# A transformer block on one core: where moving weights lie in SBUF, modulo 256 bytes

## The chip, the core and the metric

The kernel runs on one core of a Trainium2 chip. The metric is the device time of one execution in microseconds (us). Engines are named as in the profile: PE is the matmul engine (TensorE), PEld its loading of stationary operands, ACT is ScalarE, DVE VectorE, POOL GpSimd, SP SyncE. A matmul has a stationary operand (128x128 here, loaded by an instruction LDWEIGHTS) and a moving operand (up to 512 columns), and accumulates into a PSUM bank.

## The reference

One block of a hybrid encoder on 256 rows of width 2048, in float32. Cut to its matrix products:

```python
mem_n = rms_norm(mem, mem_norm_g)
h = rms_norm(x, norm_g[l, 0])
q, k, v, g, lr, u_f, u_h, u_s = jnp.split(h @ w_in[l], split_at, axis=-1)
mix = jnp.concatenate([y_a, y_b, y_c, y_d], axis=-1)
x = x + mix @ w_out[l]
x = x + cross_attention(rms_norm(x, norm_g[l, 1]), mem_n, w_xq[l], w_xkv[l], w_xo[l])
x = x + swiglu(rms_norm(x, norm_g[l, 2]), w_gate_up[l], w_down[l])
return rms_norm(x, final_norm_g)
```

y_a to y_d are four mixers of a quarter of the width each: gated linear attention, a Fourier transform, long convolutions and a short convolution. The products with weights (w_in, w_xkv, w_out, w_xq, w_xo, w_gate_up with 2 x 5632 columns, w_down) make up nearly all of the work.

## The kernel before

**Three products for one.** Every float32 operand a is split into a high part (rounded to the type float32r) and the rest: a = ah + al. A product of two is taken as ah bh + al bh + ah bl, in float32r.

**The stream of weights.** All weights lie in one array W in the order of use: blocks of 128x128, sixteen to a slab of 128x2048 (1 MB), loaded by one DMA from SP into one of three buffers `raw`. `Stream._half` (line 77) takes half a slab, 8 blocks: ACT casts it to `wh` (line 104), DVE subtracts to get `wl` (line 105). `Stream.take` hands out the parts, two or three halves ahead of their use. The tiles `wh` and `wl` have 1088 columns of 4 bytes, of which 1024 are used, from column `at` on (lines 99 to 101). `at` is 0 for blocks in the ranges `ROWS` and 8 for all others.

**Two forms of product.**

- Weights stationary (`mm`, line 304, and `gemm`): wh is loaded, and the activation's slot, 512 columns of which 256 are the high part and 256 the rest, moves past it (line 311); then wl with the high part alone (line 312). A narrow variant splits the first into two of 256 columns (lines 308 and 309).
- Weights moving (`part_rows`, line 353, and `gemm_rows`), called row products below: 128 columns of the activation's high part are loaded and 512 columns of wh move (line 356), then the same with wl (line 357), then the activation's rest with wh (line 358). It is used for the values of the cross-attention, for the values of the gated linear attention, for gate and up, and for down: `ROWS` (line 39) holds their block numbers, 256 + 64 + 2112 = 2432 of 4032. A call for 4 blocks makes 6 matmuls.

**The end.** The last 32 blocks (`HELD`) are not put into the buffers wh and wl but into 16 tiles `held` of their own (lines 88 to 97), in a pool `hp` that `mlp` opens after gate and up (line 752), so that the last products of down can run first for the upper rows and then for the lower ones.

**Places.** Every tile has an address in its SBUF partition. `gap` (line 215) allocates some bytes that nobody uses, so that what follows lies elsewhere; there are several such gaps. In the compiled program of before, the starts of the tiles that matter are, modulo 256 bytes:

| tile | role | remainder |
|---|---|---|
| act, f, oex (activation slots, 2048 bytes each) | stationary in row products, moving past stationary weights | 128 |
| wh, wl (4352 bytes each, 17 x 256) in all 8 buffers, column 0 | moving in row products | 192 |
| wh, wl from column 8 on (32 bytes) | stationary | 224 |
| held (2048 bytes each, after a gap of 64 bytes) | moving | 192 |
| tabh, tabl, backh, backl, hs (Hyena's tables and filters) | stationary on lines 987, 1055, 1056 | 64 |
| w3h, w3l (2048 bytes each) | moving on lines 987, 1055, 1056 | 64 |

The slices that a single matmul takes start at multiples of 512 bytes within these, so they have the remainders of the table.

**Order around it.** Work that is not a weight product (convolutions, attention, norms) is put between the products by a planner (`Background`), which estimates times of PE and DVE; it doesn't depend on addresses. Hyena's transforms are such work: `triple` (line 984) issues three matmuls on line 987, moving w3h, w3l, w3h past stationary tabh, tabh, tabl, each 512 columns wide, and `dft` calls it twice in a row; lines 1055 and 1056 issue two matmuls with w3h and w3l past hs. They stand between the matmuls of row products.

Of the kernel before, what the change touches and what calls it, by code (L numbers as in the profile page):

```python
# [38 lines left out]
ROWS = ((256, 512), (704, 768), (NBLK - 48 * FT, NBLK))  # L39
# [23 lines left out]
class Stream:  # L63
# [13 lines left out]
    def _half(self):  # L77

        nc, n = self.nc, 8 * len(self.halves)
        if n % 16 == 0:  # L80
            self.raw = self.rawp.tile([P, 2048], F32, name="raw", tag="raw")
            for a, b in zip(CUTS[n], CUTS[n][1:]) if n in CUTS else [(0, 1024), (1024, 2048)] if self.after else [(0, 2048)]:
                (nc.scalar if (n, a) == (0, 0) else nc.sync).dma_start(self.raw[:, a:b], self.W[n // 16][:, a:b])
                if self.after:
                    self.after.pop(0)()
        o = (n % 16) * P
        r = self.raw[:, o:o + 1024]
        if n >= NBLK - HELD:
            parts = []
            for a in (0, 512):  # L90
                wh, wl = self.places.pop(0)
                nc.scalar.copy(wh, r[:, a:a + 512])
                nc.vector.tensor_tensor(out=wl, in0=r[:, a:a + 512], in1=wh.bitcast(F32), op=ALU.subtract)
                parts.append((wh, wl))
            self.bg.dve(1024)
            self.halves.append(parts)
            return
        pool = self.extra if self.extra and len(self.halves) % 4 == 3 else self.wp
        wh, wl = (pool.tile([P, 1088], F32R, name=t, tag=t) for t in ("wh", "wl"))
        at = 0 if any(a <= n < b for a, b in ROWS) else 8  # L100
        wh, wl = wh[:, at:at + 1024], wl[:, at:at + 1024]
        edges = [0, 256, 512, 1024] if n == 0 else [0, 512, 1024] if n == 8 else [0, 1024]
        for a, b in zip(edges, edges[1:]):
            nc.scalar.copy(wh[:, a:b], r[:, a:b])  # L104
            nc.vector.tensor_tensor(out=wl[:, a:b], in0=r[:, a:b], in1=wh[:, a:b].bitcast(F32), op=ALU.subtract)  # L105
        self.bg.dve(1024)
        self.halves.append((wh, wl))
# [60 lines left out]
class Block:  # L168
# [576 lines left out]
    def mlp(self):  # L745
        tc, nc, act = self.tc, self.nc, self.act
        with tc.tile_pool(name="fp", bufs=1) as fp:
            self.gap(fp, 192)
            f = act[4:12] + [fp.tile([P, 512], F32R, name=f"f{i}") for i in range(20)] + self.h3
            with tc.tile_pool(name="gp", bufs=2) as gp:  # L750
                self.gate_up(gp, f)
            with tc.tile_pool(name="hp", bufs=1) as hp:
                self.gap(hp, 64)
                held = [hp.tile([P, 512], F32R, name=f"held{i}") for i in range(HELD // 2)]
                self.st.places = list(zip(held[0::2], held[1::2]))
                self.down(f)
# [705 lines left out]
```

## Time and profile before

| | us |
|---|---|
| median of 3 runs | 1491.95 (1491.54 to 1491.97) |
| the profiled execution, its own time | 1492.38 |
| its span in the trace | 1490.6 |
| mean granted clock of TensorE | 0.998 of full |
| DMA, mean over the span | 205 GB/s |

The page gives busy times for each engine, the chain of work that ended last, and groups of instructions: line, engine, operation, what it writes and reads by the program's names (`pg<-wh,act` is written to a PSUM bank pg from wh and act), shapes, count, busy time and mean duration. The span's time counts from 0. Matmuls are pipelined: one starts before the one ahead of it has ended by its record, so the distance from start to start, called pace below, is shorter than the duration, and the sum of durations is more than the time that they take. In the order of time, each row has start, duration, engine, line and operands.

### The profile page before, as it was taken

To read this page: it belongs to the slowest core of one execution; us is meant where nothing else is said; L and a number is where in the kernel's file an instruction comes from. 1 tells how busy PE (TensorE), PEld (TensorE's weight loads), DVE (VectorE), ACT (ScalarE), POOL (GpSimd) and SP (SyncE) were. 2 spreads that over 40 slices of the span, in tenths; PEclk is the share of its full clock that TensorE was granted. 3 is DMA by queue.
4 is the path that set the end of the run, shared out by engine and by line. 5 is a ranking of instruction groups with operands and counts; after the bars stand their busy time and mean duration, and the time that the engine had idled before them with its cause. 6 is when DMAs were issued, how large, how long until landed. Compare 5 with 4: busy or idle time off the path is not lost.

```text
span 1490.6 us, 19837 instructions
## 1 busy us (share of the span) xinstructions
PE 1479.3 (99%) x7586; PEld 1254.6 (84%) x7586; DVE 942.3 (63%) x1379; ACT 767.6 (51%) x1147; POOL 150.1 (10%) x260
## 2 busy tenths in 40 slices
PE   9999999999999999999999999999999999999997
PEld 8888888899899888888888888888888888888886
DVE  6687768778777777877765554555555456444444
ACT  6566655458555556756544444444444445434344
POOL 0100100000000001100052410111110112000000
PEclk9999999999999999999999999999999999999999
DMA  9966554454446555544567766666666666555554
GB/s 348 361 248 210 199 193 164 168 188 145 163 150 228 188 196 205 192 151 170 197 198 241 231 215 218 221 213 218 215 213 212 211 217 230 188 187 191 197 197 141
DMA packets 56174, 306.11 MB, mean 205 GB/s; under 512 B 9197, under 2 KB 10510, under 8 KB 24464
## 3 DMA queue, kind: packets, MB, share of 16 engines
q1 hardware_dynamic: 45632, 281.11, 54.3%
q0 software_dynamic: 10016, 23.08, 4.9%
q8 instruction: 59, 0.97, 0.3%
q10 hardware_dynamic: 432, 0.66, 0.1%
q14 instruction: 35, 0.29, 0.1%
HBM read 291.18 MB, written 13.63 MB: 204 GB/s over the span
## 4 chain that ended last, share of the span: by engine, by line
PE 96%; ACT 1%; DVE 1%; DMA 0%; issue 0%; SPq 0%; ACTq 0%
PE pg L311 21%; PE pg L357 17%; PE pg L358 17%; PE pg L356 17%; PE pg L312 11%; PE pm L357 1%; PE pm L356 1%; PE pm L358 1%; PE pm L987 1%; PE pm L311 1%; PE pg L308 1%; PE pg L309 1%; PE pm L738 1%; PE pm L711 0%; PE pm L312 0%; DMA raw<-in_W 0%
## 5 line engine op out<-in xcount | busy, mean ns | idle before, releaser
L105 DVE TENSOR_TENSOR wl<-raw,wh 128x1024 fp32r<-128x1024 f32 (+1 forms) x503 | 611.8, 1218 | 476.8 <-ACT wh L104 470.1
L104 ACT CAST wh<-raw 128x1024 fp32r<-128x1024 f32 (+1 forms) x503 | 525.1, 1045 | 584.2 <-PE pg L358 397.9
L311 PE MATMUL pg<-act,wh 128*128 128x512 f32 x1296 | 456.0, 394 | 1.1 <-ACT wh L104 0.9
L312 PE MATMUL pg<-act,wl 128*128 128x256 f32 x1472 | 412.2, 280 | 0.2 <-DVE wl L105 0.2
L358 PE MATMUL pg<-wh,act 128*128 128x512 f32 x1008 | 396.1, 393 | 0.0
L357 PE MATMUL pg<-wl,act 128*128 128x512 f32 x1008 | 395.7, 393 | 0.0
L356 PE MATMUL pg<-wh,act 128*128 128x512 f32 x1008 | 392.7, 390 | 0.0
L311 PEld LDWEIGHTS pg<-act,wh 128*128 128x128 f32 x1296 | 243.3, 188 | 54.7 <-ACT wh L104 1.4
L312 PEld LDWEIGHTS pg<-act,wl 128*128 128x128 f32 x1472 | 276.8, 188 | 1.5 <-DVE wl L105 0.5
L356 PEld LDWEIGHTS pg<-wh,act 128*128 128x128 f32 x1008 | 189.2, 188 | 43.5 <-issue 0.4
L357 PEld LDWEIGHTS pg<-wl,act 128*128 128x128 f32 x1008 | 189.3, 188 | 42.6
L358 PEld LDWEIGHTS pg<-wh,act 128*128 128x128 f32 x1008 | 189.4, 188 | 38.7
L780 POOL DMA_DIRECT2D hidden<-u x88 | 57.1, 656 | 311.6 <-DVE u L777 310.1
L308 PE MATMUL pg<-act,wh 128*128 128x256 f32 x176 | 50.0, 284 | 0.0
L309 PE MATMUL pg<-act,wh 128*128 128x256 f32 x176 | 49.5, 281 | 0.0
L357 PE MATMUL pg<-wl,f 128*128 128x512 f32 x120 | 47.3, 394 | 0.0
L356 PE MATMUL pg<-wh,f 128*128 128x512 f32 x120 | 47.0, 392 | 0.0
L358 PE MATMUL pg<-wh,f 128*128 128x512 f32 x120 | 46.6, 388 | 0.0
L196 DVE TENSOR_TENSOR tmp<-pg,tmp 128x256 f32<-128x256 f32 x86 | 36.0, 419 | 8.4 <-ACT tmp L318 6.6
L824 POOL DMA_DIRECT2D xrows<-tmp x48 | 27.7, 586 | 130.0 <-DVE tmp L821 126.2
L318 ACT COPY tmp<-pg 128x256 f32<-128x256 f32 x85 | 30.9, 365 | 9.5 <-PE pg L312 8.3
L308 PEld LDWEIGHTS pg<-act,wh 128*128 128x128 f32 x176 | 33.3, 189 | 0.1
(285 smaller groups left out, 1253.0 us busy)
## 6 DMA issues: line engine op xcount, KB each, us to landing
raw<-in_W SPq DMA_DIRECT2D x246, 1024.0 KB, 4.9
raw<-in_W SPq DMA_DIRECT2D x11, 512.0 KB, 7.5
hidden<-u POOLq DMA_DIRECT2D x88, 64.0 KB, 3.0
tmp<-hidden POOLq DMA_DIRECT2D x44, 128.0 KB, 4.2
res<-in_xT SPq DMA_DIRECT2D x8, 512.0 KB, 5.8
k<-in_mem SPq DMA_DIRECT2D x8, 256.0 KB, 7.8
k<-in_x SPq DMA_DIRECT2D x8, 256.0 KB, 9.4
keys<-tmp POOLq DMA_DIRECT2D x16, 128.0 KB, 5.7
```

The source lines that it names most:

```text
L104: nc.scalar.copy(wh[:, a:b], r[:, a:b])
L105: nc.vector.tensor_tensor(out=wl[:, a:b], in0=r[:, a:b], in1=wh[:, a:b].bitcast(F32), op=ALU.subtract)
L196: self.nc.vector.tensor_tensor(out=out, in0=a, in1=b, op=op)
L308: self.nc.tensor.matmul(p[:, 0:R], wh, slot[:, 0:R], start=start, stop=False)
L309: self.nc.tensor.matmul(p[:, 0:R], wh, slot[:, R:512], start=False, stop=False)
L311: self.nc.tensor.matmul(p[:, :], wh, slot[:, :], start=start, stop=False)
L312: self.nc.tensor.matmul(p[:, 0:R], wl, slot[:, 0:R], start=False, stop=stop)
L318: self.nc.scalar.copy(t, p[:, R:512])
L356: self.nc.tensor.matmul(p[:, :], hi, wh, start=start, stop=False)
L357: self.nc.tensor.matmul(p[:, :], hi, wl, start=False, stop=False)
L358: self.nc.tensor.matmul(p[:, :], lo, wh, start=False, stop=stop)
L780: nc.gpsimd.dma_start(to[:, :, 32 * a:32 * a + 32], u[32 * a:32 * a + 32, :].rearrange("f (b t) -> f b t", t=32))
```

## The change

The weights that move start at column 48 instead of 0 of their buffers, which is 192 bytes further on: remainder 192 + 192 = 384, that is 128 modulo 256, as act and f have. The gap of 64 bytes ahead of the held tiles is dropped, which brings them from remainder 192 to 128 too. Weights that stay stationary keep column 8. The buffers keep their size; the order of instructions is as before.

```diff
@@ -97,7 +97,7 @@
         pool = self.extra if self.extra and len(self.halves) % 4 == 3 else self.wp
         wh, wl = (pool.tile([P, 1088], F32R, name=t, tag=t) for t in ("wh", "wl"))
-        at = 0 if any(a <= n < b for a, b in ROWS) else 8
+        at = 48 if any(a <= n < b for a, b in ROWS) else 8
         wh, wl = wh[:, at:at + 1024], wl[:, at:at + 1024]
@@ -750,7 +750,6 @@
             with tc.tile_pool(name="hp", bufs=1) as hp:
-                self.gap(hp, 64)
                 held = [hp.tile([P, 512], F32R, name=f"held{i}") for i in range(HELD // 2)]
```

## The prediction

> **What bounds the kernel now.** I read the page first: busy times, then the chain that ended last, then the groups by line.
>
> ```profile
> span 1490.6 us, 19837 instructions
> PE 1479.3 (99%) x7586; PEld 1254.6 (84%) x7586; DVE 942.3 (63%) x1379; ACT 767.6 (51%) x1147; POOL 150.1 (10%) x260
> ...
> PE 96%; ACT 1%; DVE 1%; DMA 0%; issue 0%; SPq 0%; ACTq 0%
> PE pg L311 21%; PE pg L357 17%; PE pg L358 17%; PE pg L356 17%; PE pg L312 11%; PE pm L357 1%; PE pm L356 1%; PE pm L358 1%; PE pm L987 1%; PE pm L311 1%; PE pg L308 1%; PE pg L309 1%; PE pm L738 1%; PE pm L711 0%; PE pm L312 0%; DMA raw<-in_W 0%
> ```
>
> TensorE is busy for 99% of the span and is 96% of the chain. Nothing but its own pace can move the end by much, and lines 356 to 358, the products in which weights move, are over half of that chain. Those are the matmuls whose moving operand the change shifts; lines 311 and 312, where the weights are stationary, keep their place. How many there are, from the groups by line with shapes kept apart:
>
> ```profile
> L358 PE MATMUL pg<-wh,act 128*128 128x512 f32 x1008 | 396.1, 393 | 0.0
> ...
> L358 PE MATMUL pg<-wh,f 128*128 128x512 f32 x120 | 46.6, 388 | 0.0
> ...
> L358 PE MATMUL pm<-wh,f 128*128 128x512 f32 x40 | 15.5, 388 | 0.0
> ...
> L358 PE MATMUL pm<-wh,act 128*128 128x512 f32 x32 | 12.4, 388 | 0.0
> ...
> L358 PE MATMUL pm<-held,act 128*128 128x512 f32 x16 | 6.2, 388 | 0.0
> ```
>
> 1008 + 120 + 40 + 32 + 16 = 1216 on line 358, and as many on 356 and 357: 3648 matmuls. Their pace, start to start, from the order of time in the middle of the gate and up products (first and last of ten rows):
>
> ```profile
> 999.46 0.39 PE L358 MATMUL pg<-wh,act 128*128 128x512 f32 x1
> ...
> 1001.52 0.39 PE L358 MATMUL pg<-wh,act 128*128 128x512 f32 x1
> ```
>
> Nine steps in 2.06 us: 228.9 ns each. So 3648 of them are 835 us, and **each nanosecond on the pace is 3.65 us at the end**, with no idle time of the engine to absorb it. The recorded durations overlap; they have a resolution of 1 ns, and I use them to compare paces. First the groups of a long stretch (850 to 1200 us), then those of another (1251 to 1399 us):
>
> ```profile
> L358 PE MATMUL pg<-wh,act 128*128 128x512 f32 x511 | 201.3, 394 | 0.0
> L357 PE MATMUL pg<-wl,act 128*128 128x512 f32 x510 | 199.9, 392 | 0.0
> L356 PE MATMUL pg<-wh,act 128*128 128x512 f32 x510 | 197.9, 388 | 0.0
> ```
>
> ```profile
> L357 PE MATMUL pg<-wl,f 128*128 128x512 f32 x119 | 46.9, 394 | 0.0
> L356 PE MATMUL pg<-wh,f 128*128 128x512 f32 x119 | 46.6, 392 | 0.0
> L358 PE MATMUL pg<-wh,f 128*128 128x512 f32 x119 | 46.2, 388 | 0.0
> ```
>
> The same three durations, 388, 392 and 394, stand on other lines in the two stretches. They belong to no operand: they are a beat of three steps that the engine falls into. Their mean is 391.3, 162.4 above the pace of 228.9. And they are the same for act and f, for six or eight different buffers and for the held places, all at different addresses but with one remainder to 256, the moving tile 64 bytes above the stationary one. So if addresses matter at all, it is through that remainder, and the change sets it from 64 to 0.
>
> **The change, part by part.** No instruction, DMA, wait or byte is added or removed.
>
> (1) The casts of line 104 and subtractions of line 105 write 192 bytes further on. Their durations at the two places that the program already uses (remainder 192 where weights move, 820 to 1240 us, then 224 where they are stationary, 390 to 440 us):
>
> ```profile
> L104 ACT CAST wh<-raw 128x1024 fp32r<-128x1024 f32 x153 | 161.1, 1053 | 228.6 <-PE pg L358 228.6
> ...
> L104 ACT CAST wh<-raw 128x1024 fp32r<-128x1024 f32 x13 | 13.7, 1052 | 15.9 <-PE pg L311 11.1 <-issue 4.7
> ```
>
> 1053 and 1052 ns: the place of the write costs nothing that shows, and ScalarE stands idle until line 358 frees a buffer. I take 0. If each of these 300-odd casts took 50 ns longer, TensorE would still cover it, since one half of a slab holds 12 matmuls, 2.7 us, against 1.05.
>
> (2) The held tiles move down by 64 bytes in a pool that nothing else follows. They feed 16 x 3 = 48 of the 3648 matmuls; they are counted with the rest.
>
> (3) The 3648 matmuls with remainder 0. The trace has this case: on line 987 the moving w3h and w3l and the stationary tables lie alike (both have remainder 64), with the same shape, set between row products. One burst of six, in order of time, and its groups by line:
>
> ```profile
> 126.61 0.40 PE L358 MATMUL pg<-wh,act 128*128 128x512 f32 x1
> 126.85 0.39 PE L987 MATMUL pm<-w3h,tabh 128*128 128x512 f32 x1
> 127.08 0.40 PE L987 MATMUL pm<-w3l,tabh 128*128 128x512 f32 x1
> ...
> 128.01 0.39 PE L987 MATMUL pm<-w3h,tabl 128*128 128x512 f32 x1
> 128.23 0.39 PE L356 MATMUL pg<-wh,act 128*128 128x512 f32 x1
> ```
>
> ```profile
> L987 PE MATMUL pm<-w3l,tabh 128*128 128x512 f32 x2 | 0.8, 395 | 0.0
> L987 PE MATMUL pm<-w3h,tabh 128*128 128x512 f32 x2 | 0.8, 394 | 0.0
> L358 PE MATMUL pg<-wh,act 128*128 128x512 f32 x1 | 0.4, 398 | 0.0
> L987 PE MATMUL pm<-w3h,tabl 128*128 128x512 f32 x1 | 0.4, 389 | 0.0
> ```
>
> The first five have a successor that also lies at remainder 0 (while one matmul runs, the next one's weights are read, so I count by the pair). By starts: 126.85 to 128.01, 1.16 us, 232.0 ns, or 3.1 above 228.9. By durations: (2 x 395 + 2 x 394 + 389) / 5 = 393.4, 2.1 above 391.3. All six, the last one running into the old remainder: 126.85 to 128.23, 230.0 ns, 1.1 above. I take **2.4 ns**, between the first two and nearer to the durations, which are finer. As bounds: from below the shortest duration that any such pair shows, 388 (the first row of the next fence), 3.3 under the mean; from above the 398 in the seam at line 358, 6.7 over it.
>
> Sum: 3648 x 2.4 = 8.8 us on the profiled 1492.38 (span 1490.6 and 1.8 around it), 1501.1; the median shown is 0.43 below that execution, so **1500.7**. The likeliest case's own range is 1.1 to 3.6 ns (4 to 13 us): 1496 to 1505.
>
> **A rule against it.** LDWEIGHTS takes 188 ns and runs beside the matmul before it, inside the 228.9. The Trainium skill (TensorE: Matmul & The Clock Gate, Part 2, the step on LDWEIGHTS) states that moving data and weights have independent read ports and that loading the next weights takes no read bandwidth from the running matmul; by that, remainders can't matter and the time stays at 1491.95. Its gap for 512 columns, 215.7 ns, is 13 ns under this trace's 228.9, which speaks for something between the two reads that the rule leaves out.
>
> **The rivals.**
>
> *It locks to a faster beat* (not slower). Five steps don't show the steady beat, and which one is reached may depend on the phase of entry. Lines 1055 and 1056 also have remainder 0 within each pair:
>
> ```profile
> L1055 PE MATMUL pm<-w3h,hs x8: 388/392/393, 104.4 to 154.4; 128*128 128x512 f32 x8
> ...
> L1056 PE MATMUL pm<-w3l,hs x8: 388/398/398, 104.6 to 154.6; 128*128 128x512 f32 x8
> ```
>
> One time in eight both took 388. If remainder 0 stays there, each matmul gains 3.3 ns: 3648 x 3.3 = 12 us, 1480. It decides as soon as a product in the long stretch runs more than a few dozen steps without falling out of 388. Against it: the medians of these two rows, 392 and 398, and the five counted on line 987. 13 in 100.
>
> *The remainder doesn't matter*, and the bursts of line 987 only show a beat disturbed at the seam (the 398 just before them): 1492. For it: five steps are few, and the first of them follows that seam. Against it: five steps in a row with a mean of 393.4, where the beat of the row products gives 391.3 over any three. 7 in 100.
>
> *It locks to a slower beat.* The row products themselves ran so once, early on:
>
> ```profile
> 102.04 0.40 PE L358 MATMUL pg<-wh,act 128*128 128x512 f32 x1
> ...
> 103.90 0.40 PE L357 MATMUL pg<-wl,act 128*128 128x512 f32 x1
> ```
>
> Eight steps in 1.86 us: 232.5 ns, every duration 0.40. Were that the lock, with a rounding error of about 1 ns, 3.6 to 4.6 ns x 3648 = 13 to 17 us: 1505 to 1509. 15 in 100. The forecast has the remaining 65.
>
> **How the numbers follow.** Slower: 65 + 15 = 80 in 100. No change, within 0.2% (3 us, about what a measurement of this kernel can tell from none): 7. Faster: 13. The range runs from 1491, which takes in the case of no change, to 1508; it leaves out the fast beat and the edge of the slow one.
>
> **What would show it.** Lines 356 to 358 in the long stretches should have durations whose mean is about 393.7 instead of 391.3, in a beat other than 388, 392, 394; lines 311, 312 and the times of casts and subtractions should stand; the whole added time should lie in the stages of row products in proportion to their matmuls (2112 of 2432 blocks in the last 700 us, so some 7.6 of the 8.8 us there). A mean of 391.3 again means that the remainder is nothing; a mean of 388 the fast beat; idle time ahead of line 356 released by lines 104 or 105 would mean that I missed a cost of the writes.

## The result and the profile after

| | before | after |
|---|---|---|
| median, us | 1491.9 (1491.53 to 1492.09, 6 runs) | 1484.7 (1483.97 to 1485.15, 6 runs) |
| the profiled execution | 1492.38 | 1483.97 |
| its span | 1490.6 | 1482.2 |

The ratio is 0.9952, 95% interval 0.9939 to 0.9965: 7.2 us faster, the interval 5.2 to 9.1. The forecast was slower by 8.8 us, with 1491 as its lower end: the sign was wrong.

From the page of the kernel after, the span, the busy times and the chain by engine:

```profile
span 1482.2 us, 19837 instructions
PE 1471.8 (99%) x7586; PEld 1254.9 (85%) x7586; DVE 942.1 (64%) x1379; ACT 766.3 (52%) x1147; POOL 150.1 (10%) x260
...
PE 96%; ACT 1%; DVE 1%; issue 0%; DMA 0%; SPq 0%; ACTq 0%; DVEq 0%
```

The bound is where it was, and the number of instructions too; TensorE has lost 7.5 us of busy time, the others next to nothing (ScalarE 1.3, VectorE 0.2). The groups by line in the long stretch from 850 to 1200 us, which showed 388, 392 and 394 before (the last column but one is the mean duration in ns):

```profile
L356 PE MATMUL pg<-wh,act 128*128 128x512 f32 x516 | 200.7, 389 | 0.0
L357 PE MATMUL pg<-wl,act 128*128 128x512 f32 x515 | 200.3, 389 | 0.0
L358 PE MATMUL pg<-wh,act 128*128 128x512 f32 x515 | 200.3, 389 | 0.0
```

Three different durations have become one. The pace, from the order of time, with the first and the last of 1676 steps in the kernel after, and in the second fence the first and last of 1662 steps in the kernel before:

```profile
819.81 0.39 PE L356 MATMUL pg<-wh,act 128*128 128x512 f32 x1
...
1199.70 0.39 PE L358 MATMUL pg<-wh,act 128*128 128x512 f32 x1
```

```profile
820.01 0.39 PE L357 MATMUL pg<-wl,act 128*128 128x512 f32 x1
...
1200.42 0.39 PE L357 MATMUL pg<-wl,act 128*128 128x512 f32 x1
```

379.89 / 1676 = 226.67 ns after, 380.41 / 1662 = 228.89 before. The difference, 2.22 ns, times 3648 is 8.1 us, against 8.4 between the two spans and 7.2 between the medians. Added up from start to start over the whole trace, the row products take 836.0 us before and 828.4 after; all the rest of TensorE's time differs by 0.9. So the gain is in the row products, and it is their pace. That it is 7.5 us and not 8.1 has a reason in the same traces: the short runs of only twelve row products between other work got slower, 230.2 ns a step against 229.5 to 229.8 before, since the new pace is reached only after some steps.

### The profile page after: what moved, and what is told of

It is laid out like the page before. It is cut to its first block, busy times and chain, and to the rows that moved or that the text cites. A ratio compares the mean times of both kernels' runs of the same rounds, so it can differ in the third digit from the quotient of the medians.

```text
span 1482.2 us, 19837 instructions
## 1 busy us (share of the span) xinstructions
PE 1471.8 (99%) x7586; PEld 1254.9 (85%) x7586; DVE 942.1 (64%) x1379; ACT 766.3 (52%) x1147; POOL 150.1 (10%) x260
## 4 chain that ended last, share of the span: by engine, by line
PE 96%; ACT 1%; DVE 1%; issue 0%; DMA 0%; SPq 0%; ACTq 0%; DVEq 0%
PE pg L311 21%; PE pg L356 17%; PE pg L357 17%; PE pg L358 17%; PE pg L312 11%; PE pm L357 1%; PE pm L356 1%; PE pm L358 1%; PE pm L311 1%; PE pm L986 1%; PE pg L308 1%; PE pg L309 1%; PE pm L738 1%; PE pm L312 1%; PE pm L711 0%; ACT wh L104 0%
```

## The experiments

Below, the difference of a matmul is the place of its moving tile less that of the stationary one, modulo 256 bytes: 64 for row products before, 0 after, 0 on line 987. The questions were: why the bursts of line 987, at difference 0, ran at 231 to 232 ns where 3648 row products at difference 0 run at 226.67; whether it is the difference of the two places that counts; which part of the edit did it; and whether there is a better place.

**The burst made longer.** In the kernel before, each group of three on line 987 is issued six times; a repeat starts the sum anew.

```diff
-            self.triple(p, th, tl, hi, lo, True, True)
+            for _ in range(6):
+                self.triple(p, th, tl, hi, lo, True, True)
```

> The kernel before, with the six matmuls of line 987 replaced by 36 in a row (each group of three issued six times; the repeats restart the sum, so the result is the same). Moving and stationary tiles have the same remainder there. Theory (a row of such matmuls needs some ten steps after another remainder until it locks, and then runs at 226.7 ns, that is durations of 388 to 389): the first five to ten steps of each burst have a mean near 231 ns as in the kernel before, and the rest 226.7. Rival (line 987 has a pace of its own, and the changed kernel's gain has another cause): 231 ns to the end of each burst. The time rises by some 10 bursts x 30 x 0.23 = 70 us in both.

One of these bursts in the order of time:

```profile
126.27 0.40 PE L358 MATMUL pg<-wh,act 128*128 128x512 f32 x1
126.51 0.39 PE L987 MATMUL pm<-w3h,tabh 128*128 128x512 f32 x1
126.74 0.40 PE L987 MATMUL pm<-w3l,tabh 128*128 128x512 f32 x1
126.97 0.39 PE L987 MATMUL pm<-w3h,tabl 128*128 128x512 f32 x1
127.20 0.40 PE L987 MATMUL pm<-w3h,tabh 128*128 128x512 f32 x1
127.43 0.39 PE L987 MATMUL pm<-w3l,tabh 128*128 128x512 f32 x1
127.67 0.39 PE L987 MATMUL pm<-w3h,tabl 128*128 128x512 f32 x1
...
128.80 0.39 PE L987 MATMUL pm<-w3l,tabh 128*128 128x512 f32 x1
```

The groups of the same burst from 127.98 us on:

```profile
L987 PE MATMUL pm<-w3h,tabl 128*128 128x512 f32 x11 | 4.3, 389 | 0.0
L987 PE MATMUL pm<-w3h,tabh 128*128 128x512 f32 x10 | 3.9, 389 | 0.0
L987 PE MATMUL pm<-w3l,tabh 128*128 128x512 f32 x10 | 3.9, 389 | 0.0
```

The first five steps take 1.16 us, 232 ns each, as they did before: in the trace's own ns, finer than these rows, they are 230, 236, 228, 232, 231. The next five, 127.67 to 128.80, take 1.13, 226 ns each, and the rest stays at 389, the duration that all row products have in the changed kernel. Every burst of 36 does so, after five to seven steps. The rival falls: line 987 has no pace of its own. The five steps on which the forecast rests were the whole way into the beat, and nothing of the beat itself. The trace of the kernel before had this too: in each of its eight bursts of six that follow a row product, the five steps are 230, 235 or 236, 228 or 229, 232 or 233, and 231 ns, and the sixth is 226. (The time was 1546.51 us, 54 more; the guess of 70 counted two bursts too many.)

**All places in one run.** The changed kernel, with the weights' first column stepped through eight places in stretches.

```diff
+        if 1152 <= n < 1920:
+            at = 8 * ((n - 1152) // 96)
+        elif 1920 <= n < 3328:
+            at = 8 * ((n - 1920) // 176)
```

> The changed kernel, with the starting column of the weights stepped through 0, 8, ..., 56 (32 bytes each) in eight stretches of gate and up (moving weights, 264 matmuls each) and in eight stretches of the products of w_out, w_xq and w_xo (stationary weights, 96 pairs each). Theory (the pace depends on the difference of the two places modulo 256 bytes, in steps of 32, and each difference locks to a beat whose sum is a whole number of some 6.67 ns, 8 cycles of 1.2 GHz): gate and up run at 228.9 ns at column 0, at 226.7 at column 48, at other fixed beats between 225 and 238 elsewhere; the pairs of stationary products run at 346.7 ns per pair at column 8 and at other fixed values elsewhere. Rival (only equal places are special, everything else is alike): 226.7 at column 48 and 228.9 at all seven others. Time within 10 us of the changed kernel's 1484.7.

Three stretches of gate and up by groups: column 8 (822 to 878 us), column 16 (883 to 938) and column 48 (1130 to 1186):

```profile
L361 PE MATMUL pg<-wl,act 128*128 128x512 f32 x81 | 32.3, 399 | 0.0
L360 PE MATMUL pg<-wh,act 128*128 128x512 f32 x81 | 31.9, 394 | 0.0
L362 PE MATMUL pg<-wh,act 128*128 128x512 f32 x80 | 31.4, 392 | 0.0
```

```profile
L361 PE MATMUL pg<-wl,act 128*128 128x512 f32 x79 | 31.2, 395 | 0.0
```

```profile
L360 PE MATMUL pg<-wh,act 128*128 128x512 f32 x83 | 32.3, 389 | 0.0
```

The pace by place, one stretch for each, from start to start over the second half of the stretch (for the pairs, over whole beats of its longest part without other work); a pair is one matmul of 512 columns and one of 256:

| difference, bytes | 0 | 32 | 64 | 96 | 128 | 160 | 192 | 224 |
|---|---|---|---|---|---|---|---|---|
| row products, ns | 226.7 | 233.3 | 228.9 | 233.3 | 233.3 | 234.3 | 233.3 | 233.3 |
| stationary weights, ns per pair | 353.3 | 346.7 | 348.9 | 350.0 | 351.1 | 346.7 | 353.3 | 353.3 |

The rival falls: 228.9 was itself a good place, and most others are at 233.3. The pairs have two best places, one of which (160) they had. For them difference 0, the best of the row products, is among the worst. The whole run took 1498.53 us, 14 more than the changed kernel, where 10 had been the most expected.

**The same difference at another place.** Activation slots 64 bytes further on, moving weights back at column 0, stationary ones at 24; the gaps of the other pools follow by 64 bytes, so that every difference stays.

```diff
+        self.gap(cp, 64)
         self.act = [cp.tile([P, 512], F32R, name=f"act{i}") for i in range(24)]
...
-        at = 48 if any(a <= n < b for a, b in ROWS) else 8
+        at = 0 if any(a <= n < b for a, b in ROWS) else 24
```

> The activation slots (act, f, oex) lie 64 bytes further on, at remainder 192; weights that move start at column 0 again, remainder 192; stationary weights at column 24, so that every difference between moving and stationary is that of the changed kernel, at places 64 bytes higher; held tiles at 192. Theory (the difference counts): row products at 226.7 ns, time 1484 to 1486. Rival (the place of the moving weights counts, 128 good and 192 bad): 228.9 ns and 1492.

From 850 to 1200 us:

```profile
L357 PE MATMUL pg<-wl,act 128*128 128x512 f32 x516 | 200.7, 389 | 0.0
```

1484.77 us (1484.46 to 1484.9), 0.9951 of the kernel before (0.9935 to 0.9968). The moving weights lay at remainder 192, where the kernel before had them; the time is that of the changed kernel. The difference counts, the place doesn't. That it counts modulo 256 shows too: the eight buffers lie multiples of 256 bytes apart and share one pace, while differences 0 and 128 have different ones.

**The held tiles alone as before.**

```diff
+                self.gap(hp, 64)
                 held = [hp.tile([P, 512], F32R, name=f"held{i}") for i in range(HELD // 2)]
```

> The changed kernel with the gap of 64 bytes ahead of the held tiles kept, so that their 48 matmuls run at a difference of 64 again. Theory: their durations are 388, 392, 394 in a beat of three, 2.2 ns more than 389, so 0.1 us in all, not to be seen in the time (1484 to 1486); all other row products as in the changed kernel. Rival (the held tiles' place shifts something larger, such as a wait at the end): a microsecond or more at the end of the trace.

```profile
L358 PE MATMUL pm<-wh,f 128*128 128x512 f32 x40 | 15.6, 389 | 0.0
L356 PE MATMUL pm<-held,act 128*128 128x512 f32 x16 | 6.3, 394 | 0.0
L358 PE MATMUL pm<-held,act 128*128 128x512 f32 x16 | 6.3, 393 | 0.0
L357 PE MATMUL pm<-held,act 128*128 128x512 f32 x16 | 6.2, 389 | 0.0
```

The 48 fall back, to a mean of 392, though not to the expected beat of 388, 392 and 394; the other row products keep 389 but for a few beside them, at 390. The one run took 1485.17 us, 0.02 above the slowest of the changed kernel's six, so the microsecond of the rival doesn't show. The second edit is worth about a tenth of a microsecond by the durations; the first does the rest.

**Places between.**

```diff
+        if 1152 <= n < 1920:
+            at = (4, 6, 10, 12, 36, 38, 42, 44)[(n - 1152) // 96]
+        elif 1920 <= n < 3328:
+            at = (44, 46, 50, 52, 4, 60, 20, 36)[(n - 1920) // 176]
```

> The changed kernel with starting columns that are no multiples of 8: in gate and up 44, 46, 50, 52, 4, 60, 20, 36 by stretch (differences to the stationary tile of -16, -8, +8, +16, 80, 48, 144 and 208 bytes), in the products of w_out, w_xq and w_xo 4, 6, 10, 12, 36, 38, 42, 44. Theory (the grain is 32 bytes, places within one are alike except where a line of 32 bytes is straddled): no stretch is faster than the whole multiples, so none of the row products is under 226.7 ns and no pair under 346.7; those within 16 bytes of difference 0 run between 226.7 and 233.3. Rival (the grain is finer, and there are better places between): some stretch of row products under 226.2, or some pair under 346. Time 1484 to 1500.

The stretch at column 44, 16 bytes short of difference 0 (768 to 800 us):

```profile
L360 PE MATMUL pg<-wh,act 128*128 128x512 f32 x45 | 18.0, 400 | 0.0
```

In the order of the columns, the row products ran at 236.7, 231.6, 232.8, 231.7, 231.1, 233.3, 233.3 and 234.7 ns; the best pair, at column 44, at 346.7. None of these places is faster than 226.7 for a row product or 346.7 for a pair. The time was 1499.88 us. That part of the theory held; the bound of 233.3 for places near difference 0 did not: 16 bytes under it is the slowest place of all.

**The rest of the weights alone.** wh stays, wl is stepped (`wl[:, to:to + 1024]`, with `to` as `at` in the first sweep).

> The changed kernel with wl alone stepped through columns 0, 8, ..., 56 in the same eight stretches each, wh staying at 48 (moving) and 8 (stationary). Theory (each matmul's pace follows from its own difference, its successor's and the phase on a grid of 8 cycles): 226.7 ns for row products where wl is at 48, 228 to 234 elsewhere; pairs 346.7 at column 8, as much or more elsewhere. Rival (a mixture of places finds a shorter beat than one place for both): row products under 226.2 or pairs under 346. Time 1484 to 1500.

Row products: 226.7 with wl at column 48, 228.9 at column 32, 231 to 233.3 at the six others; no pair under 346.7. A mixture of places brings no shorter beat. 1494.88 us.

**Half a load of weights.** In the changed kernel the second of three row products takes 64 stationary columns.

```diff
-        self.nc.tensor.matmul(p[:, :], hi, wl, start=False, stop=False)
+        self.nc.tensor.matmul(p[0:64, :], hi[:, 0:64], wl, start=False, stop=False)
```

> The changed kernel with 64 instead of 128 stationary columns in the second matmul of each three of a row product (line 357): it leaves out the rest of the weights for the lower 64 of each 128 rows. Theory (what a matmul takes beyond 256 cycles of 1.2 GHz is the time of reading the next weights, one cycle for each 32 bytes of a partition: 16 for 128 columns, 8 for 64): 673.3 ns per three instead of 680, time 8.1 us less than the changed kernel, 1476 to 1478. Rival (the excess is a fixed cost of each matmul, whatever is loaded): 680 ns per three and 1484 to 1486.

The groups from 850 to 1200 us:

```profile
L358 PE MATMUL pg<-wh,act 128*128 128x512 f32 x509 | 199.5, 392 | 0.0
L357 PE MATMUL pg<-wl,act 128*64 128x512 f32 x508 | 199.4, 392 | 0.0
L356 PE MATMUL pg<-wh,act 128*128 128x512 f32 x508 | 198.3, 390 | 0.0
```

Both readings fall. The kernel became slower: 1495.39 us, 229.8 ns a step, 689.3 per three. Less to load took more time here, so what that theory counts as reading the next weights is neither a price by the byte nor a fixed one. The single-step beat of difference 0 did not survive one unlike load in three; in its place stands one that repeats after 15 steps (3446.67 ns). Why, this run does not tell.

**A worse difference throughout.** Column 16 and a gap of 128 bytes ahead of the held tiles.

```diff
-        at = 48 if any(a <= n < b for a, b in ROWS) else 8
+        at = 16 if any(a <= n < b for a, b in ROWS) else 8
...
+                self.gap(hp, 128)
```

> The changed kernel with weights that move at column 16 and a gap of 128 bytes ahead of the held tiles, so that every row product has a difference of 128 bytes. Theory (the steady beat of the sweep, 233.3 ns at this difference, holds for all 3648 row products, and the time follows at 3.65 us per nanosecond): 4.4 ns over the kernel before, 16 us, 1506 to 1509; durations at the end, held tiles included, with a mean near 395.8. Rival (the stretches of the sweep were short, or gate and up differ from the other products): less than 10 us over the kernel before.

The first and the last of 1635 steps, and the three groups from 850 to 1200 us:

```profile
820.03 0.40 PE L356 MATMUL pg<-wh,act 128*128 128x512 f32 x1
...
1199.98 0.39 PE L356 MATMUL pg<-wh,act 128*128 128x512 f32 x1
```

```profile
L358 PE MATMUL pg<-wh,act 128*128 128x512 f32 x503 | 198.5, 395 | 0.0
L356 PE MATMUL pg<-wh,act 128*128 128x512 f32 x503 | 198.4, 395 | 0.0
L357 PE MATMUL pg<-wl,act 128*128 128x512 f32 x502 | 198.1, 395 | 0.0
```

1506.2 us, 1.0092 of the kernel before (1.0075 to 1.0109): 14.3 us slower by the medians, 13.1 by the profiled executions, and the rival falls. But 379.95 / 1635 = 232.4 ns, not the 233.3 of the sweep at the same difference: 3.5 ns over the kernel before and 12.8 us by the sum, of 16 expected. The time lay in the expected range, the pace under it. Difference 128 has at least two beats, so the difference alone gives its pace to within about a nanosecond. Difference 64 may have a second one too: the slow steps of the kernel before that the prediction shows from 102.04 us on belong to nine of 233.3 ns each (101.80 to 103.90), where its long stretches run at 228.9; nine steps are too few to call them steady. What chooses between beats is open.

No kernel of these is faster than the changed one.

## Why the prediction was wrong

- **What bounds, and the price of a nanosecond: right.** 3648 matmuls on TensorE's chain, 3.65 us per ns. Three kernels bear it out: 2.22 ns less (8.1 us by the sum) and 7.2 us less, the same with everything shifted, 3.5 ns more (12.8 us by the sum) and 14.3 us more. From start to start, the row products of the profiled executions took 7.5 us less and 12.3 us more.
- **Only the remainder counts: right, and more exactly the difference.** The kernel with both places moved by 64 bytes shows it. The rule of the Trainium skill on independent read ports (TensorE: Matmul & The Clock Gate, Part 2, the step on LDWEIGHTS) gives no room for it. Here the pace of one and the same matmul went from 226.7 to 236.7 ns with nothing changed but the place, so that rule does not cover this kernel's loads and matmuls; which of the two reads waits, and for what, the runs don't show. Nor do they tell whether a matmul's own stationary tile counts or the next one's: in every steady stretch both lie alike.
- **Casts and subtractions: right.** Line 104 took 1047 ns at the new place against 1053, line 105 1223 against 1224.
- **The step that failed: (3), the 2.4 ns more for each row product.** It took the mean of the five steps on line 987 as the pace of a steady stretch. The longer burst showed that these five are the way in, and that from the sixth on the same pair of tiles runs at a duration of 389, as the row products of the changed kernel do. In place of 2.4 ns more, the runs showed 2.2 ns less: 226.67 against 228.89. The sixth step of the burst that the prediction shows (128.01 to 128.23 us) was already one of 226 ns; it was set aside because its successor lies at another remainder. The prediction had said that the durations 388, 392 and 394 belong to a beat and to no operand, and that five steps don't show the steady beat; it then used them as if they did. The row products in the changed kernel have such a way in too, wherever other work stands between them; in the order of time after a matmul of Hyena's filters:

```profile
116.34 0.39 PE L356 MATMUL pg<-wh,act 128*128 128x512 f32 x1
...
118.65 0.39 PE L357 MATMUL pg<-wl,act 128*128 128x512 f32 x1
...
120.91 0.39 PE L358 MATMUL pg<-wh,act 128*128 128x512 f32 x1
```

The first ten steps take 2.31 us, 231 ns each; the next ten 2.26, 226 ns. The last four of the ten, 236, 228, 233 and 231 in the trace's own ns, are nearly those of line 987.

- **The rival that came true: the faster beat, at 13 in 100.** Its mechanism was right, down to the point from which it decides, though not dozens of steps but five to ten are needed. Its price was too high, 12 us: it took the shortest single duration, 388, for the beat, and that is 389, which makes 2.2 ns of 3.3. The one time in eight in which lines 1055 and 1056 both took 388 pointed to it, though two steps show a beat no better than five.
- **The range.** It reached down to no change and stopped there; since the fast beat could not be told from the five steps, its 8 us should have been inside.

## What to carry to other kernels

The pace of a short burst can be that of its way in, and nothing of the steady one. Where the engine's steps repeat in a beat over long stretches, look for a long stretch, or make one, before pricing a change of it. Where every matmul loads new weights, the difference of the two operands' places modulo 256 bytes is worth over 4% of the pace (226.7 to 236.7 ns here): step it through in one run, by stretches, for each form of product on its own, since the best place of one form was among the worst of another. The best place pays only in runs longer than the way in: those of twelve lost by it here.

## What the hardware showed beyond that

The steady beats add up to whole multiples of 6.667 ns: one step of 226.67 is 34 of them; three steps at difference 64 are 686.67, 103; two at difference 128 in the sweep are 466.67, 70; seven of 232.38 in the last experiment are 1626.67, 244; the 15 steps with half a load in three are 517; two pairs of stationary products at difference 160 are 693.33, 104. So starts come back to the same phase of some cycle, and a beat is a way around it; that fits the observation that one difference can have two beats. One stretch leaves the unit open: with wl alone at column 40, every pair of stationary products takes 350.0 ns, which is 52.5, and only two pairs make a whole number. What that cycle is, and why difference 0 closes in a single step of 34 where places 16 or 32 bytes away take longer, the runs don't show. They also don't show a difference at which a matmul of 512 columns with a load beside it runs steadily under 226.67 ns.
